# Contiguous first transfers, dt's one-source steps on ScalarE, and a two-phase transfer rate in the planner of a hybrid SSD and attention layer

## The chip, the cores and the metric

The kernel runs on one core of a Trainium2 chip. The metric is device time of one execution in microseconds (us); lower is better. The times are medians of several runs.

The engines are named as the profile names them: PE is TensorE (matmuls and transposes), DVE is VectorE, ACT is ScalarE, POOL is GpSimd, SP is SyncE, which here only issues transfers.

## The reference

One layer of a bidirectional encoder over 512 tokens of 1024 channels, float32. Cut to what matters:

```python
h = rmsnorm(x, pre_mix_norm)
z, xbc, dt_raw, q, k, v, gates = split_cols(h @ w_in, IN_SPLITS)   # 2048, 4096, 64, 1024, 256, 256, 2048
# SSD branch, chunks of 128 tokens, a scan forward and one backward, 32 heads each
xbc = silu(depthwise_conv(xbc) + conv_b)
dt  = softplus(dt_raw + dt_bias)             # 512 tokens x 64 (two directions)
cs  = cumsum(dt * -exp(a_log)) in each chunk # decay tables come from cs
y_ssd = gated_rmsnorm(y_fwd + y_bwd + xs * d_skip, z, ssd_norm) @ w_ssd_out
# attention, 16 query heads, 4 key heads, window +-128, relative bias, a sink logit for each head
y_attn = window_attention(q, k, v, sink, rel_bias_table) @ w_attn_out
mixed = (sigmoid(g_ssd) * y_ssd + sigmoid(g_attn) * y_attn) @ w_o
x = x + rmsnorm(mixed, post_mix_norm)
f = square(relu(rmsnorm(x, pre_mlp_norm) @ w_mlp_in)) @ w_mlp_out
out = x + rmsnorm(f, post_mlp_norm)
```

The part of the kernel that the change touches is the beginning: the norm's scale, the V and dt columns of the first projection, softplus and the sums over dt.

## The kernel before

**Products.** Every float32 operand of a large product is split into a high and a low part that PE can take at full rate. For a weight tile `wr` of 128x1024, ACT casts the high part `wh` (L496) and POOL subtracts to get the low part `wl` in four instructions of 128x256 (L500). A product is then three matmuls (`mm3`): high by high, low by high, high by low. All matmuls stand on line L421 and all transposes on L425, which are helpers.

**Stages at the start.** `start` (L637) loads the tokens in two forms. `xt` is a transposed copy of the first 256 tokens, in eight pieces k of 128 channels by 256 tokens; ACT and DVE multiply each by the norm's weight `gT` (L661, L663) to `xg`, and PE forms V and dt of the first two token tiles from it in plain float32, before the row scales exist. `x` is the tokens by row in eight transfers (L679); ACT (L687) and DVE (L688) form sums of squares, POOL the row scale (L690, L691), ACT and DVE the scaled tokens (L724, L725), and PE transposes those of the last two tiles. For the first two, PE spreads the row scales over the partitions by a product with a diagonal tile `dg`, and the split parts `h` follow on DVE (L707), ACT (L709) and POOL (L710). `v_quanta` loads the V and dt columns `wv` in three pieces of 2, 3 and 3 k (`V_CHUNKS`), the first on ACT's queue and the others on SP's (L584), and splits them (L588, L591).

**Softplus.** `dt_math` (L777) works on 128x256 tiles named `dtw`: max(v, 0) + log(1 + exp(-|v|)), the logarithm by a series in s = e / (e + 2). The steps are |v| and exp on ACT (L787, L788), e + 2 (L789), its reciprocal (L790), the product (L791), the square (L792), the first factor 1/17 (L793), seven Horner steps (L795), a last one (L796), max(v, 0) (L797), dt (L798) and dt by -exp(a_log) (L800), all on DVE. `sums` follows: cumulative sums by PE, a copy `cs` (L810), its negative `ncs` (L811), the decay tables (L813 to L816).

**After them.** `kv_quanta` projects K, of which ACT makes `KH` (L848, L850) and DVE `KL` (L849); `q_quantum` makes Q (L875 on ACT, L876 on DVE). Attention for each key head k is scores (L899 on DVE), maximum (L905), exp (L908), sums (L909 to L911), division (L914), transposes `pT` (L925). Each conv block of the SSD branch is four DVE steps (L976) and a silu (L982, L983). `L1147` multiplies the masks `m` of the scan, and the scan's outputs are products of `m` and `x`.

**Order.** The instructions are first written by quanta, then `Planner.plan` runs a model of the engines over all of them: durations by shape, a lock between DVE and POOL, and one queue of transfers with a rate. It takes for each engine the instruction that is ready and due first, and PE's order comes out of it too, within rules. `chain` then fixes the order so found on every engine. A tile's free buffer counts as well: three raw weight tiles, three split ones, three PE banks named `pp` and five named `ps`. The transfers in the model:

```python
                queue = max(queue, t + 900) + size / RATE
                free[e], end = end, queue + LAND
```

Here `t` is the time of issue in ns, `RATE` is 340 bytes for each ns, and `LAND` 2500 ns.

Of the kernel before, what the change touches and what calls it, by code (L numbers as in the profile page):

```python
# [12 lines left out]
AF = mybir.ActivationFunctionType  # L13
ALU = mybir.AluOpType
# [8 lines left out]
C_Z, C_X, C_B, C_C, C_DT = 0, 2048, 4096, 5120, 6144  # L23
C_Q, C_K, C_V, C_GS, C_GA = 6208, 7232, 7488, 7744, 8768
# [9 lines left out]
BACK = 3  # L34
WARM = 8
V_CHUNKS = ((0, 2), (2, 5), (5, 8))
COLD = 7000.0
RATE, LAND = 340, 2500

OUTPUT = 350  # L40

# [23 lines left out]
def packed(given):  # L65

    rows = lambda n: given[n].reshape(-1, 128)
    by_partition = lambda a: np.ascontiguousarray(a.reshape(8, 128, -1).transpose(1, 0, 2).reshape(128, -1))
    cv = np.concatenate([rows(n) for n in ("conv_w", "conv_b", "b_gate", "ssd_norm", "pre_mlp_norm")]).T
    row = np.concatenate([given[n].reshape(-1) for n in ("dt_bias", "a_log", "attn_sink", "d_skip")])  # L70
    bucket, far = buckets()
    bias = np.ascontiguousarray(given["rel_bias_table"][bucket].T)
    bias[:, far] = NEG
    w = given["w_in"][0]
    return {"cv": np.ascontiguousarray(cv), "row": row, "bias": bias,
            "gt": np.ascontiguousarray(rows("pre_mix_norm").T), "xt": by_partition(given["x"][0, :256].T),
            "wv": by_partition(np.concatenate([w[:, C_V:C_V + 256], w[:, C_DT:C_DT + 64]], axis=1))}


class Slots:  # L80
# [5 lines left out]
    def get(self, name, shape=(128, 512), dtype=F32):  # L86
        s = self.free.popleft()
        self.n += 1
        t = self.pool.tile(list(shape), dtype, tag=f"s{s}", name=f"{name}_{self.n}", bufs=1)
        self.tags[t.tensor.name] = f"s{s}", 1  # L90
        self.slot[id(t)] = (s, t)
        return t
# [6 lines left out]
class Planner:  # L99
# [184 lines left out]
    def plan(self, wait=0.3):  # L284
        late = self.deadlines()
        left = [len(p) + len(q) for p, q in zip(self.pre, self.turn)]
        ready = [0.0] * len(self.ins)
        done = [math.inf] * len(self.ins)
        avail = {e: [] for e in self.OVERLAP}
        key = [n if self.eng[n] == "PE" else late[n] for n in range(len(self.ins))]  # L290
        for n, k in enumerate(left):
            if not k:
                avail[self.eng[n]].append(n)
        free = dict.fromkeys(self.OVERLAP, 0.0)
        port = {"DVE": 0.0, "POOL": 0.0}
        queue, kind, landed = 0.0, None, deque([0.0] * 8)
        order = {e: [] for e in self.OVERLAP}
        for _ in self.ins:
            best = None
            for e, some in avail.items():  # L300
                if some:
                    t = max(free[e], min(ready[n] for n in some))
                    if best is None or t < best[0]:
                        best = t, e
            t, e = best
            some = avail[e]
            if e == "PE":
                n = self.next_matmul(some, ready, done, t, kind)
            else:
                n = min((n for n in some if ready[n] <= t), key=lambda n: (key[n], n))  # L310
                m = min(some, key=lambda n: (key[n], n))
                if ready[m] <= t + wait * self.cost[n][0]:
                    n = m
            some.remove(n)
            order[e].append(n)
            t = max(t, ready[n])
            c, locks = self.cost[n]
            if e == "PE" and t < COLD:
                c *= 2
            end = t + c  # L320
            if e == "SP" or "DMA" in type(self.ins[n]).__name__:
                aps = self.operands(self.ins[n].outs)
                size = 4 * math.prod(d[1] for d in aps[0].ap)
                queue = max(queue, t + 900) + size / RATE
                free[e], end = end, queue + LAND
                landed.append(end)
                landed.popleft()
                free["SP"] = max(free["SP"], min(landed) + 60)
            elif e == "PE":
                end += self.change(kind, self.kind[n])  # L330
                kind = self.kind[n]
                free[e], end = end, end + 160
            else:
                if locks:
                    other = "POOL" if e == "DVE" else "DVE"
                    end += max(0.0, port[other] - t - 145)
                    port[e] = end
                free[e] = end - self.OVERLAP[e]
            done[n] = end
            for s in self.post[n]:  # L340
                same = self.eng[s] == e == "PE"
                ready[s] = max(ready[s], free[e] if same else end + self.AFTER[self.eng[s]])
                left[s] -= 1
                if not left[s]:
                    avail[self.eng[s]].append(s)
            for s in self.next[n]:
                ready[s] = max(ready[s], t)
                left[s] -= 1
                if not left[s]:
                    avail[self.eng[s]].append(s)  # L350
        self.length = max(free.values())
        return order
# [10 lines left out]
class Trunk:  # L363
# [204 lines left out]
    def v_quanta(self):  # L568

        nc = self.nc  # L570
        get = self.slots.get
# [4 lines left out]
        def chunk(k0, k1):  # L576
            kk = k1 - k0
            raw = []

            def loads():  # L580
                r = self.wp.tile([128, 1024], F32, tag="wr", name=self.name("wr"), bufs=RAW)
                self.tags[r.tensor.name] = "wr", RAW
                raw.append(r[:, :kk * 320].rearrange("p (k n) -> p k n", k=kk))
                (nc.sync if k0 else nc.scalar).dma_start(r[:, :kk * 320], self.d_wv[:, k0 * 320:k1 * 320])  # L584

            def make():
                hi, lo = (t[:, :kk * 320].rearrange("p (k n) -> p k n", k=kk) for t in self.weight_parts())
                nc.scalar.copy(hi, raw[0])  # L588
                for k in range(kk):
                    e = nc.vector if k % 2 == 0 else nc.gpsimd  # L590
                    e.tensor_tensor(lo[:, k], raw[0][:, k], hi[:, k].bitcast(F32), op=ALU.subtract)  # L591
                return raw[0], hi, lo

            return loads, make, False
# [42 lines left out]
    def start(self):  # L637
        nc = self.nc
        get, put = self.slots.get, self.slots.put
        self.gT = self.const("gT", [128, 8])  # L640
        nc.scalar.dma_start(self.gT, self.d_gt)
        self.ident = self.const("ident", [128, 128])
        self.at(0, lambda: nc.scalar.dma_start(self.ident, self.d_cst[:, :128]))
        self.mhalf = self.const("mhalf", [128, 1])
        nc.vector.memset(self.mhalf, -0.5)
        self.ssq0 = self.const("ssq0", [128, 8])
        self.rst0 = self.const("rst0", [128, 4])
        ones = self.const("ones0", [128, 128])
# [2 lines left out]
        for _ in range(WARM):  # L651
            self.mm(pg[:, :128], ones, ones, True, True)
        self.h = [(get("h", dtype=F32R), get("h", dtype=F32R)) for _ in range(8)]
        xt, xg = ([get(n) for _ in range(4)] for n in ("xt", "xg"))
        cols = lambda a: [a[k // 2][:, k % 2 * 256:(k % 2 + 1) * 256] for k in range(8)]
        self.xg, xs = cols(xg), cols(xt)
        for k in range(8):
            if k % 2 == 0:
                nc.sync.dma_start(xt[k // 2], self.d_xt[:, k * 256:(k + 2) * 256])
            if k % 2:  # L660
                nc.scalar.activation(self.xg[k], xs[k], AF.Copy, scale=self.gT[:, k:k + 1])  # L661
            else:
                nc.vector.tensor_scalar(self.xg[k], xs[k], self.gT[:, k:k + 1], None, op0=ALU.mult)  # L663
        put(*xt)
        for t in range(2):
            xt = self.load_tokens(t)
# [110 lines left out]
    def dt_math(self):  # L777
# [8 lines left out]

        nc.scalar.activation(e, v, AF.Abs)  # L787
        nc.scalar.activation(e, e, AF.Exp, scale=-1.0)  # L788
        nc.vector.tensor_scalar(r, e, 2.0, None, op0=ALU.add)  # L789
        nc.vector.reciprocal(r, r)  # L790
        nc.vector.tensor_tensor(e, e, r, op=ALU.mult)  # L791
        nc.vector.tensor_tensor(s2, e, e, op=ALU.mult)  # L792
        nc.vector.tensor_scalar(p, s2, 1.0 / 17, None, op0=ALU.mult)  # L793
        for n in (15, 13, 11, 9, 7, 5, 3):
            nc.vector.scalar_tensor_tensor(p, p, 1.0 / n, s2, op0=ALU.add, op1=ALU.mult)  # L795
        nc.vector.scalar_tensor_tensor(p, p, 1.0, e, op0=ALU.add, op1=ALU.mult)  # L796
        nc.vector.tensor_scalar(v, v, 0.0, None, op0=ALU.max)  # L797
        nc.vector.scalar_tensor_tensor(self.dt, p, 2.0, v, op0=ALU.mult, op1=ALU.add)  # L798
        nc.scalar.activation(bias[:, 1], bias[:, 1], AF.Exp)
        nc.vector.scalar_tensor_tensor(al, self.dt, -1.0, bias[:, 1].unsqueeze(1).to_broadcast([128, 4, 64]),  # L800
# [2 lines left out]
        def sums():  # L803
# [4 lines left out]
            pt = self.bank("ps")  # L808
            self.mm(pt[:, :256], self.ones, al, True, True)
            nc.vector.tensor_copy(self.cs, pc3)  # L810
            nc.vector.tensor_scalar(self.ncs, self.cs, -1.0, None, op0=ALU.mult)  # L811
            pt3 = pt[:, :256].rearrange("p (c h) -> p c h", c=4)
            nc.scalar.activation(self.dec, pt3, AF.Exp)  # L813
            nc.vector.tensor_tensor(self.coef, pt3, self.cs, op=ALU.subtract)
# [885 lines left out]
```

## Time and profile before

| | us |
|---|---|
| median of 3 runs | 1090.57 |
| lowest, highest | 1088.97, 1091.22 |
| the profiled execution's own time | 1093.82 |
| its span in the trace | 1092.0 |

The granted PE clock of the profiled execution is 0.998 of full speed. Over the span PE is busy for 98%, POOL for 73%, DVE for 69%, ACT for 58%, and the core moves 122 GB/s on average, 267 GB/s in the first fortieth of the span.

A row of the timeline reads: start, duration, engine, line, operation, what it writes and reads with shapes, how many instructions were joined in the row, and in brackets how long the engine stood idle before it and who released it. A row of a line's summary gives the least, the median and the greatest duration in ns. A row of PE's waits gives who waited for whom: sum, times, longest. Several engines work at once, so an idle engine costs time only if PE, which is the fullest, has to wait in the end.

### The profile page before, as it was taken

The numbers are of one execution on the slowest core, as the hardware profiler recorded it, in microseconds if no ns is written. First come the engines' busy times: TensorE is split into PE (matmuls) and PEld (weight loads), VectorE is DVE, ScalarE is ACT, GpSimd is POOL, SyncE is SP. The second block draws the span as 40 slices with busy tenths as digits, with TensorE's granted clock in tenths as the row PEclk, the third lists the DMA queues.
The fourth block names the chain that finished last, engine by engine and source line by source line (L and its number), as shares of the span: only waits on it lengthen the run. The fifth ranks groups of instructions, "written<-read, shape, count | busy, mean of one in ns | idle before, by whom it ended". The sixth has DMA issues, their size and how long they took to land.

```text
span 1092.0 us, 16583 instructions
## 1 busy us (share of the span) xinstructions
PE 1072.8 (98%) x5542; PEld 896.6 (82%) x5542; DVE 755.2 (69%) x1284; ACT 637.7 (58%) x1372; POOL 799.0 (73%) x986
## 2 busy tenths in 40 slices
PE   8998999999999999999999999999999999999997
PEld 7787888888888888787888888888888888888885
DVE  5877788787687687888787753334572583583698
ACT  6556777686676777676678533323654544444552
POOL 4736566567658798988989976521588898898994
PEclk9999999999999999999999999999999999999999
DMA  8334433534445536354645563534222422424232
GB/s 267 99 94 128 126 88 103 147 91 121 114 105 135 138 101 165 99 148 122 170 127 142 148 187 108 162 102 161 83 75 69 149 83 82 149 81 139 98 97 77
DMA packets 208181, 133.20 MB, mean 122 GB/s; under 512 B 9688, under 2 KB 190168, under 8 KB 208096
## 3 DMA queue, kind: packets, MB, share of 16 engines
q1 hardware_dynamic: 207664, 131.75, 43.0%
q8 instruction: 43, 0.70, 0.3%
q10 hardware_dynamic: 432, 0.40, 0.1%
q14 instruction: 42, 0.34, 0.1%
HBM read 127.63 MB, written 4.49 MB: 121 GB/s over the span
## 4 chain that ended last, share of the span: by engine, by line
PE 85%; DVE 6%; DMA 5%; ACT 2%; issue 1%; POOL 1%; SPq 0%; DVEq 0%; POOLq 0%; ACTq 0%
PE pp L421 59%; PE ps L421 23%; PE ps L425 3%; DMA rstd<-rrow 2%; DMA rf<-csT 1%; DVE yT L1219 1%; DVE dtw L797 1%; DVE u L976 1%; DMA wr<-in_wv 1%; DMA rrow<-rcol 1%; DMA rcol<-rrow 1%; ACT wh L496 0%; DVE m L1146 0%; DVE dtw L795 0%; SPq L1119 0%
## 5 line engine op out<-in xcount | busy, mean ns | idle before, releaser
L500 POOL TENSOR_TENSOR wl<-wr,wh 128x256 fp32r<-128x256 f32 (+1 forms) x500 | 421.4, 871 | 154.8 <-ACT wh L496 141.4
L421 PE MATMUL pp<-h,wh 128*128 128x512 f32 (+1 forms) x1712 | 524.9, 388 | 1.4 <-ACT KH L850 1.4
L421 PEld LDWEIGHTS pp<-h,wh 128*128 128x128 f32 x1712 | 316.2, 188 | 65.7 <-ACT KH L850 1.9
L421 PE MATMUL pp<-h,wl 128*128 128x512 f32 (+1 forms) x856 | 331.9, 388 | 0.0
L496 ACT CAST wh<-wr 128x1024 fp32r<-128x1024 f32 x131 | 136.4, 1041 | 141.7 <-PE pp L421 119.8
L421 PEld LDWEIGHTS pp<-h,wl 128*128 128x128 f32 x856 | 160.8, 188 | 32.0 <-issue 0.2
L1536 POOL TENSOR_TENSOR wl<-wd,wh 128x256 fp32r<-128x256 f32 x158 | 129.8, 859 | 12.1 <-ACT wh L1533 12.0
L1533 ACT CAST wh<-wd 128x512 fp32r<-128x512 f32 x82 | 47.3, 618 | 30.1 <-PE ps L421 15.8
L421 PE MATMUL ps<-wh,fl 128*128 128x512 f32 x164 | 63.8, 389 | 0.0
L421 PE MATMUL ps<-wl,fh 128*128 128x512 f32 x164 | 63.8, 389 | 0.0
L421 PE MATMUL ps<-wh,fh 128*128 128x512 f32 x164 | 63.8, 389 | 0.0
L1144 ACT ACTIVATE n<-cb,tables 128x128 f32<-128x128 f32 x128 | 49.4, 390 | 19.0 <-DVE cb L1135 16.8
L1403 DVE SCALAR_TENSOR_TENSOR pp<-pp,r 128x512 f32<-128x512 f32 (+1 forms) x31 | 17.6, 567 | 57.0 <-ACT r L1400 56.8
L976 DVE SCALAR_TENSOR_TENSOR u<-pp,cv,u 128x510 f32<-128x510 f32 (+1 forms) x64 | 47.7, 745 | 6.7 <-ACT u L972 5.4
L1145 ACT ACTIVATE m<-cb,tables 128x128 f32<-128x128 f32 x128 | 49.0, 388 | 3.9 <-DVE cb L1135 3.9
L421 PE MATMUL pp<-yh,wl 128*128 128x512 f32 x128 | 49.9, 390 | 0.0
L421 PE MATMUL pp<-yl,wh 128*128 128x512 f32 x128 | 49.8, 389 | 0.0
L421 PE MATMUL pp<-yh,wh 128*128 128x512 f32 x128 | 49.7, 389 | 0.0
L1140 ACT ACTIVATE rf<-rf,tables 128x128 f32<-128x128 f32 x128 | 42.3, 391 | 12.6 <-DMA rf<-csT 12.6
L908 ACT ACTIVATE P<-P,mx 128x384 f32<-128x384 f32 (+1 forms) x64 | 35.2, 552 | 18.4 <-DVE mx L905 18.4
L1138 POOL TENSOR_TENSOR rb<-rb,tables 128x512 f32<-128x512 f32 x32 | 33.6, 1054 | 14.7 <-DMA rb<-csT 10.9
L1074 POOL TENSOR_TENSOR xd<-x,tables 128x256 f32<-128x256 f32 x48 | 33.5, 719 | 12.0 <-ACT x L999 10.1
(269 smaller groups left out, 2170.9 us busy)
## 6 DMA issues: line engine op xcount, KB each, us to landing
wr<-in_w_in SPq DMA_DIRECT2D x74, 512.0 KB, 4.1
wr<-in_w_mlp_in SPq DMA_DIRECT2D x32, 512.0 KB, 4.1
wd<-in_w_mlp_out SPq DMA_DIRECT2D x64, 256.0 KB, 4.9
rf<-csT SPq DMA_DIRECT2D x32, 256.0 KB, 4.8
rb<-csT SPq DMA_DIRECT2D x32, 256.0 KB, 3.9
wr<-in_w_ssd_out SPq DMA_DIRECT2D x14, 512.0 KB, 4.2
E<-csE SPq DMA_DIRECT2D x96, 64.0 KB, 3.5
x<-in_x SPq DMA_DIRECT2D x16, 256.0 KB, 5.3
```

The costliest lines, as they stand in the source:

```text
L421: self.nc.tensor.matmul(out, lhsT, rhs, start=start, stop=stop, skip_group_check=more)
L496: self.nc.scalar.copy(hi[:, :m], raw)
L500: engines[e].tensor_tensor(lo[:, c], raw[:, c], hi[:, c].bitcast(F32), op=ALU.subtract)
L908: nc.scalar.activation(p[:, :w], p[:, :w], AF.Exp, bias=mx[:, n:n + 1], accum_out=sm[:, n:n + 1])
L976: nc.vector.scalar_tensor_tensor(u[:, a:e], ps[:, a + d:e + d], self.wtap(t, b), u[:, a:e], op0=ALU.mult, op1=ALU.add)
L1074: nc.gpsimd.tensor_tensor(v4(xd[:, d * 256:(d + 1) * 256]), v4(xs(c)), by_dir(self.coef, c)[:, d].unsqueeze(2).to_broadcast([128, 4, 64]), ...
L1138: nc.gpsimd.tensor_tensor(v4(rb), v4(rb), cs[:, 1].unsqueeze(2).to_broadcast([128, 4, 128]), op=ALU.subtract)
L1140: nc.scalar.activation(v4(rf)[:, h], v4(rf)[:, h], AF.Identity, bias=ncs[:, 0, h:h + 1])
L1144: nc.scalar.activation(v4(n)[:, h], cb[:, 0], AF.Copy, scale=dt[:, 0, h:h + 1])
L1145: nc.scalar.activation(v4(m)[:, h], cb[:, 1], AF.Copy, scale=dt[:, 1, h:h + 1])
L1533: nc.scalar.copy(hi, src)
L1536: (nc.vector if q == 512 else nc.gpsimd).tensor_tensor(lo[:, c], src[:, c], hi[:, c].bitcast(F32), op=ALU.subtract)
```

## The change

Three things are changed together.

1. `xt` and `wv` are laid out so that each transfer reads one stretch of memory. `gT`'s eight columns ride at the head of the first piece of `xt`, and `xt` comes in five pieces (1, 2, 2, 2 and 1 k) in place of four of 2. The separate transfer of `gT` on ACT's queue is gone. A small copy into `rst0` on ACT stands at the front of its row.
2. In `dt_math`, five steps with one source go from DVE to ACT: e + 2, the square, the factor 1/17, max(v, 0) and `ncs`. The constant 2.0 for the bias is a new tile `two`.
3. In `plan`, the rate is 350 for transfers issued in the first 12000 ns of the model, and 260 afterwards, in place of 340.

```diff
+X_CHUNKS = ((0, 1), (1, 3), (3, 5), (5, 7), (7, 8))
-RATE, LAND = 340, 2500
+RATE, EARLY, LAND = 260, 350, 2500
...
-                queue = max(queue, t + 900) + size / RATE
+                queue = max(queue, t + 900) + size / (EARLY if t < 12000 else RATE)
...
-                (nc.sync if k0 else nc.scalar).dma_start(r[:, :kk * 320], self.d_wv[:, k0 * 320:k1 * 320])
+                (nc.sync if k0 else nc.scalar).dma_start(
+                    r[:, :kk * 320], self.d_wv[k0 * 320 * 128:k1 * 320 * 128].rearrange("(p n) -> p n", p=128))
...
-        nc.scalar.dma_start(self.gT, self.d_gt)
+        self.two = self.const("two", [128, 1])
+        nc.vector.memset(self.two, 2.0)
...
-        xt, xg = ([get(n) for _ in range(4)] for n in ("xt", "xg"))
-        cols = lambda a: [a[k // 2][:, k % 2 * 256:(k % 2 + 1) * 256] for k in range(8)]
-        self.xg, xs = cols(xg), cols(xt)
-        for k in range(8):
-            if k % 2 == 0:
-                nc.sync.dma_start(xt[k // 2], self.d_xt[:, k * 256:(k + 2) * 256])
-            if k % 2:
-                nc.scalar.activation(self.xg[k], xs[k], AF.Copy, scale=self.gT[:, k:k + 1])
-            else:
-                nc.vector.tensor_scalar(self.xg[k], xs[k], self.gT[:, k:k + 1], None, op0=ALU.mult)
+        nc.scalar.copy(self.rst0, self.mhalf.to_broadcast([128, 4]))
+        xt, xg = ([get(n) for _ in range(m)] for n, m in (("xt", 5), ("xg", 4)))
+        self.xg = [xg[k // 2][:, k % 2 * 256:(k % 2 + 1) * 256] for k in range(8)]
+        at = 0
+        for x, (k0, k1) in zip(xt, X_CHUNKS):
+            n = (k1 - k0) * 256 + (8 if k0 == 0 else 0)
+            nc.sync.dma_start(x[:, :n], self.d_xt[at:at + 128 * n].rearrange("(p n) -> p n", p=128))
+            at += 128 * n
+            if k0 == 0:
+                nc.vector.tensor_copy(self.gT, x[:, :8])
+            for k in range(k0, k1):
+                c, g = n - (k1 - k) * 256, (self.gT[:, k:k + 1] if k else x[:, :1])
+                if k % 2:
+                    nc.scalar.activation(self.xg[k], x[:, c:c + 256], AF.Copy, scale=g)
+                else:
+                    nc.vector.tensor_scalar(self.xg[k], x[:, c:c + 256], g, None, op0=ALU.mult)
...
-        nc.vector.tensor_scalar(r, e, 2.0, None, op0=ALU.add)
+        nc.scalar.activation(r, e, AF.Identity, bias=self.two)
...
-        nc.vector.tensor_tensor(s2, e, e, op=ALU.mult)
-        nc.vector.tensor_scalar(p, s2, 1.0 / 17, None, op0=ALU.mult)
+        nc.scalar.activation(s2, e, AF.Square)
+        nc.scalar.activation(p, s2, AF.Copy, scale=1.0 / 17)
...
-        nc.vector.tensor_scalar(v, v, 0.0, None, op0=ALU.max)
+        nc.scalar.activation(v, v, AF.Relu)
...
-            nc.vector.tensor_scalar(self.ncs, self.cs, -1.0, None, op0=ALU.mult)
+            nc.scalar.activation(self.ncs, self.cs, AF.Copy, scale=-1.0)
```

The changed kernel's lines have other numbers: L797 to L816 of the kernel before are L807 to L826, and helper lines shift by two.

The order changes with it. On DVE in the softplus stage, the row before the change (`dtw` are its tiles, `KL` is the low part of K, `pp` a PE bank):

```order
L604 TENSOR_TENSOR dtw_71<-ps_294,row 128x64
L797 TENSOR_SCALAR dtw_71<-dtw_71 128x256
L789 TENSOR_SCALAR dtw_372<-dtw_371 128x256
L790 RECIPROCAL dtw_372<-dtw_372 128x256
L849 TENSOR_TENSOR KL_430<-pp_404,KH_429 64x512
L791 TENSOR_TENSOR dtw_371<-dtw_371,dtw_372 128x256
L792 TENSOR_TENSOR dtw_373<-dtw_371 128x256
L849 TENSOR_TENSOR KL_436<-pp_404,KH_435 64x512
L793 TENSOR_SCALAR dtw_374<-dtw_373 128x256
L795 SCALAR_TENSOR_TENSOR dtw_374<-dtw_374,dtw_373 128x256 x5
```

and the same place after it (L607 is L604, L859 is L849, L805 is L795):

```order
L607 TENSOR_TENSOR dtw_71<-ps_299,row 128x64
L800 RECIPROCAL dtw_377<-dtw_377 128x256
L801 TENSOR_TENSOR dtw_376<-dtw_376,dtw_377 128x256
L859 TENSOR_TENSOR KL_435<-pp_409,KH_434 64x512
L859 TENSOR_TENSOR KL_441<-pp_409,KH_440 64x512
L805 SCALAR_TENSOR_TENSOR dtw_379<-dtw_379,dtw_378 128x256 x5
```

Four DVE instructions are gone between the dt sum and the Horner steps, and both KL stand ahead of the Horner steps.

On SP at the start, the transfers before the change (`xt` transposed tokens, `wr` pieces of V's weights, `x` tokens by row):

```order
L659 DMA xt_106<-in_xt 128x512
L659 DMA xt_107<-in_xt 128x512
L584 DMA wr_150<-in_wv 128x960
L659 DMA xt_108<-in_xt 128x512
L584 DMA wr_152<-in_wv 128x960
L659 DMA xt_109<-in_xt 128x512
L679 DMA x_200<-in_x 128x512
```

and after it:

```order
L664 DMA xt_108<-in_xt 128x264
L664 DMA xt_109<-in_xt 128x512
L586 DMA wr_155<-in_wv 128x960
L664 DMA xt_110<-in_xt 128x512
L664 DMA xt_111<-in_xt 128x512
L586 DMA wr_157<-in_wv 128x960
L664 DMA xt_112<-in_xt 128x256
L689 DMA x_205<-in_x 128x512
```

The third piece of V's weights now has 264 + 3 x 512 columns of `xt` ahead of it on SP, in place of 3 x 512.

On PE at about 450 us, the row before the change (`pp` projections of `h`, `ps` with `m` and `x` outputs of the scan, `ps_5332` the transposes of the conv block B):

```order
L421 MATMUL pp_5292<-h_102,wh_5112 128x512
L421 MATMUL pp_5292<-h_103,wh_5112 128x512
L421 MATMUL pp_5292<-h_102,wl_5113 128x512
L421 MATMUL pp_5292<-h_104,wh_5112 128x512
L421 MATMUL pp_5292<-h_105,wh_5112 128x512
L421 MATMUL pp_5292<-h_104,wl_5113 128x512
L425 MATMUL ps_5332<-ident,B_5167 128x128 x4
L421 MATMUL pp_5350<-h_90,wh_5178 128x512
```

and after it (names are five higher, so `pp_5297` is `pp_5292`, and `ps_5337` is `ps_5332`):

```order
L423 MATMUL pp_5297<-h_94,wh_5117 128x512
L423 MATMUL pp_5297<-h_93,wl_5118 128x512
L423 MATMUL ps_5231<-m_5063,x_4597 64x128 x4
L423 MATMUL ps_5231<-m_5141,x_4597 64x128 x4
L427 MATMUL ps_5337<-ident,B_5172 128x128 x4
L423 MATMUL pp_5297<-h_95,wh_5117 128x512
L423 MATMUL pp_5297<-h_96,wh_5117 128x512
```

B's transposes stood behind the whole projection; now they stand behind its first six matmuls, 18 matmuls earlier, and a piece of the scan's outputs has moved next to them from 12 matmuls ahead.

More of the change, by code (lines that the diff above doesn't have):

```diff
@@ L67, in packed @@
     rows = lambda n: given[n].reshape(-1, 128)
-    by_partition = lambda a: np.ascontiguousarray(a.reshape(8, 128, -1).transpose(1, 0, 2).reshape(128, -1))
+    xt, wv = given["x"][0, :256].T.reshape(8, 128, 256), np.concatenate(
+        [given["w_in"][0][:, c:c + n].reshape(8, 128, n) for c, n in ((C_V, 256), (C_DT, 64))], axis=2)
+    pieces = lambda a, cuts: np.concatenate([a[k0:k1].transpose(1, 0, 2).reshape(-1) for k0, k1 in cuts])
     cv = np.concatenate([rows(n) for n in ("conv_w", "conv_b", "b_gate", "ssd_norm", "pre_mlp_norm")]).T
@@ L73, in packed @@
     bias[:, far] = NEG
-    w = given["w_in"][0]
+    first = np.concatenate([rows("pre_mix_norm").T, xt[0]], axis=1)
     return {"cv": np.ascontiguousarray(cv), "row": row, "bias": bias,
-            "gt": np.ascontiguousarray(rows("pre_mix_norm").T), "xt": by_partition(given["x"][0, :256].T),
-            "wv": by_partition(np.concatenate([w[:, C_V:C_V + 256], w[:, C_DT:C_DT + 64]], axis=1))}
+            "xt": np.concatenate([first.reshape(-1), pieces(xt, X_CHUNKS[1:])]), "wv": pieces(wv, V_CHUNKS)}
 class Slots:
```

## The prediction

> **What bounds the kernel now.** I read the page's shares first, then TensorE's own waits, then the timelines of the other engines around each of them.
>
> ```profile
> PE 1072.8 (98%) x5542; PEld 896.6 (82%) x5542; DVE 755.2 (69%) x1284; ACT 637.7 (58%) x1372; POOL 799.0 (73%) x986
> 6.59 9.02 PE L421 MATMUL ps<-wr,xg 128*128 128x320 f32 x32 [1.77 <-DMA wr<-in_wv]
> 15.98 0.44 PE L425 MATMUL pp<-ident,x 128*128 128x128 f32 x2 [0.37 <-ACT x L724]
> 44.49 0.72 PE L421 MATMUL pp<-h,wh 128*128 128x512 f32 x2 [1.45 <-ACT KH L850]
> 51.12 0.39 PE L421 MATMUL ps<-KH,Q 128*128 128x256 f32 x1 [0.89 <-DVE Q L876]
> 84.99 0.45 PE L421 MATMUL ps<-KH,Q 128*128 128x384 f32 x1 [2.86 <-ACT pT L925]
> ```
>
> TensorE (PE) is busy for 98% of the span, and the change leaves its matmuls as they are. So only a hole in its row can be gained, and a new hole is what can be lost. The three holes at 44, 51 and 85 us are 1.45 + 0.89 + 2.86 = 5.20. They look unrelated: one waits for K, one for Q, one for a transposed P. VectorE's (DVE's) timeline, with ScalarE (ACT) and GpSimd (POOL) beside it, shows one source for the first two:
>
> ```profile
> 25.93 5.63 POOL L710 TENSOR_TENSOR h<-hf,h 128x256 fp32r<-128x256 f32 x8
> 31.52 7.70 POOL L500 TENSOR_TENSOR wl<-wr,wh 128x256 fp32r<-128x256 f32 x11
> 30.23 0.42 ACT L788 ACTIVATE dtw<-dtw 128x256 f32<-128x256 f32 x1
> 30.23 9.13 DVE L797 TENSOR_SCALAR dtw<-dtw 128x256 f32<-128x256 f32 x1 [0.48 <-ACT dtw L787]
> 39.28 0.28 DVE L789 TENSOR_SCALAR dtw<-dtw 128x256 f32<-128x256 f32 x1
> 39.60 1.75 DVE L790 RECIPROCAL dtw<-dtw 128x256 f32<-128x256 f32 x1
> 41.27 0.62 DVE L849 TENSOR_TENSOR KL<-pp,KH 64x512 fp32r<-64x512 f32 x1
> 41.92 0.58 ACT L850 CAST KH<-pp 64x512 fp32r<-64x512 f32 x1 [7.98 <-DVE KL L849]
> ```
>
> L797 is v = max(v, 0), one source, 128x256. It lasts 9.13 us; L789, of the same operation and shape, takes 0.28. POOL runs without a gap from 25.93 until its eleven L500 splits end at 39.22, and L797 ends at 39.36. So L797 stood until POOL's queue ran dry, and 9.13 - 0.28 = 8.85 us of DVE were lost. Everything behind it is late: the reciprocal, KL at 41.27, ACT's KH (which stood for 7.98), then PE at 44.49.
>
> **dt's steps on ScalarE.** The new rows on ACT are 128x256 activations, 0.42 each by L788. DVE's L789, L792, L793, L797 and the later L811 go. Walking the stage by these durations: Exp (L788) still ends at 30.65, the relu and "+2" take ACT 2 x 0.42 to 31.5, the reciprocal takes 1.75 to 33.25, and L791, with two sources, 0.85 to 34.1. KL then follows at 34.1 in place of 41.27, and the second KL by 37.1 once ACT and PE have fed it. For the Horner steps and the rest:
>
> ```profile
> L795 DVE SCALAR_TENSOR_TENSOR dtw<-dtw,dtw x7: 424/426/852, 44.2 to 47.9; 128x256 f32<-128x256 f32 x7
> L811 DVE TENSOR_SCALAR tables<-tables x1: 816/816/816, 62.4 to 62.4; 128x256 f32<-128x256 f32 x1
> L905 DVE TENSOR_SCALAR mx<-mx x16: 154/307/686, 55.6 to 327.5; 128x4 f32<-128x4 f32 x16
> L911 DVE RECIPROCAL sm<-sm x16: 167/178/180, 59.2 to 331.2; 128x4 f32<-128x4 f32 x16
> 47.08 1.66 DVE L795 SCALAR_TENSOR_TENSOR dtw<-dtw,dtw 128x256 f32<-128x256 f32 x2
> ```
>
> A two-source step takes 0.43 alone and 0.85 with POOL at work. I take 0.85 for the five that now start at 37.1: to 41.4. Two more, L796, L798, KL and the two Q at the shown 0.7 to 0.85 put both Q at about 47.5, while PE without these holes, and with 0.3 from the start (below), reaches the scores at 51.12 - 0.89 - 1.45 - 0.3 = 48.5. So the holes of 1.45 and 0.89 both go: **2.34**. ACT's five extra rows, 2.1 us, lie where ACT stood for 7.98 and cost nothing; without that cover (the chain still late) each would delay KH by 0.42.
>
> This price rests on the stall not finding another victim. The other one-source rows beside POOL, L905 and L811, waited at most 0.53 and about 0.54 over their short time. [...]
>
> **The third hole** hangs on a chain in which DVE and ACT hand work to each other without rest:
>
> ```profile
> 53.58 0.48 DVE L899 CUSTOM_DVE_ANT_0 P<-ps,bt,row 128x256 f32<-128x256 f32 x1
> 56.30 1.04 PE L421 MATMUL ps<-dtw,cst 128*128 128x128 f32 x6
> 58.90 0.42 DVE L810 COPY tables<-ps 128x256 f32<-128x256 f32 x1
> 72.30 0.48 DVE L899 CUSTOM_DVE_ANT_0 P<-ps,bt,row 128x256 f32<-128x256 f32 x1
> 84.56 0.37 ACT L925 COPY pT<-ps 128x256 f32<-128x256 f32 x1
> ```
>
> The first score row of DVE (53.58) starts 2.46 after PE's first score matmul (51.12). With DVE free in time it would start about 0.45 behind it, one score matmul and its handover, so against PE's row the chain moves 2.0 ahead. It can't move more: L810 copies what PE wrote from 56.30 to 57.34, and stands 1.6 to 1.9 behind that now. I take **2.0** of the 2.86, leaving a hole of 0.9. The bounds are 1.7 and the whole 2.86 (L811 off DVE adds 0.82, which could fetch the rest).
>
> **The start.** The transfers' bytes ahead of the token tiles are the same within 3 KB; what changes is their cut. PE starts plain V when wv's first piece lands (6.59), which now leaves ACT's queue first.
>
> ```profile
> 5.12 1.28 ACT L661 ACT_TABLE_LOAD   x1 [5.12 <-DMA xt<-in_xt]
> 11.72 1.56 DVE L591 TENSOR_TENSOR wl<-wr,wh 128x320 fp32r<-128x320 f32 x2
> 13.21 0.68 DVE L688 CUSTOM_DVE_ANT_0 junk<-x 128x512 f32<-128x512 f32 x1
> 13.38 0.63 ACT L687 ACTIVATE junk<-x 128x512 f32<-128x512 f32 x1 [0.63 <-DMA x<-in_x]
> 0.00:20.00 20.00, 16.45 (x74) 12.52 (x75) 10.18 (x25) 11.54 (x24) 8.62 (x17) 1.00 0.91 298
> ```
>
> An earlier first matmul and the 1.28 table load taken off the way do not reach the end: at 15.98 PE waits again, for the normalised tokens, and these wait for landed x (13.38) with the transfer engines 91% busy. wv's third piece has 134 KB more of xt ahead of it than before, at 298 GB/s 0.45 us later; its DVE split (11.72) would then push L688 (13.21). Against that stands the loss of 128 small rows of gT at the head. I take 0, between 0.5 better and 0.6 worse.
>
> **The planner's rate.** With another transfer rate the planner writes 47 pieces of PE's order elsewhere, all between about 138 and 643 us apart from a few near the start. Near the start both row-scale broadcasts now stand side by side and POOL writes the eight h one split, 0.70, earlier. Eight POOL rows of 5.63 / 8 = 0.704 pace a projection:
>
> ```profile
> 26.19 1.03 PE L421 MATMUL pp<-h,wh 128*128 128x512 f32 x3
> 28.68 0.63 PE L421 MATMUL pp<-h,wh 128*128 128x512 f32 x2
> 29.39 0.63 PE L421 MATMUL pp<-h,wh 128*128 128x512 f32 x2
> 72.47 0.62 PE L421 MATMUL pp<-h,wh 128*128 128x512 f32 x2
> 73.15 0.62 PE L421 MATMUL pp<-h,wh 128*128 128x512 f32 x2
> ```
>
> A step takes 0.71 there and 0.68 elsewhere: 8 x 0.03 = 0.24, with a little at 26.19; I take **0.3**, from 0 to 0.6. The rest of the new order I cost at nothing, from 1 better to 1 worse, by these rows:
>
> ```profile
> PE ps L421 <- DVE m L1147: 1.6, 2, 1.0
> PE ps L425 <- DVE u L983: 0.9, 1, 0.9
> PE ps L425 <- DVE P L914: 0.3, 1, 0.3
> 449.20 1.14 DVE L983 SCALAR_TENSOR_TENSOR B<-th,B 128x512 f32<-128x512 f32 x1
> 454.93 0.60 PE L425 MATMUL ps<-ident,B 128*128 128x128 f32 x4
> ```
>
> All of today's waits behind 85 us are 1.6 + 0.9 + 0.3 = 2.8 in four places, 0.7 each. B's transposes, shown in the order above, move 18 rows (18 x 0.227 = 4.1 us) ahead, to about 450.8; B is ready at 450.34. That still fits, with 0.5 to spare.
>
> **Sum.** 2.34 + 2.0 + 0 + 0.3 = 4.64. The profiled execution (1093.82, of which the span is 1092.0) becomes 1089.2. It lies 3.25 above the median of 1090.57, and the same gain makes 1085.9 of the median. About 0.2%, 2.2 us, is what a measurement of this kernel can tell from no change.
>
> **Forecast, 0.64:** 1085.9. Its own range, all bad bounds (2.34 + 1.7 + 0 - 0.6 - 1 = 2.4) to all good (2.34 + 2.86 + 0.6 + 0.5 + 1 = 7.3): 1083.3 to 1088.1.
>
> **Rival, the stall takes the reciprocal, 0.09.** DVE's first instruction under POOL's unbroken row is now the one-source reciprocal at 31.5. If it waits as L797 did, it ends at 39.4 to 41.0 in place of 41.35; with two DVE steps fewer behind it (0.42 + 0.29) the chain gains 1.0 to 2.7, the first hole shrinks and the third stays: some 1.0 in all, 1089.6. Against it, L911 keeps to 167 to 180 ns everywhere, and 1753 ns for 256 elements is slow, ordinary work. [...]
>
> **Rival, the third hole is bound elsewhere, 0.11.** If ACT's casts between 60 and 84 and not DVE's lateness set 84.56, the 2.86 stays, and with 0.5 lost in the start the gain is 2.34 + 0.3 - 0.5 = 2.1: 1088.4. The continuous handover up to 84.56 speaks against it.
>
> **Rival, slower: the new order, 0.16.** PE takes its rows in order, so a piece set ahead of its producer stops everything. The planner sets margins like the 0.5 above by modelled durations; where DVE or POOL run late by a doubled step (0.43 to 0.85), such a margin is gone. If 14 of the 47 pieces wait for today's mean of 0.7, that is 9.8 in place of 2.8, 7.0 more: 7.0 - 4.64 = 2.4 slower, 1092.9. It turns from a gain at 4.64 more of waits, nine to ten places. For it: four such places exist today. Against: they came from an order drawn in the same way, and cost 2.8 in 535 us.
>
> That the change doesn't remove the stall at all is in the first rival.
>
> **Numbers.** Faster by over 0.2% (below 1088.4): the forecast and half of the third-hole case, 0.70. Within: the reciprocal case and the other half, 0.14. Slower: 0.16. The range of 1082.5 to 1090.5 holds the first three cases with their bounds and leaves out the slower one.
>
> **What would show it.** No one-source DVE row over 1 us between 30 and 40; the reciprocal near 31.5 with 1.75; KH no longer waiting for 8 us; no PE wait near 44 and 51, and about 0.9 near 80; PE's first real wait still for L724's tokens near 16. It is wrong if a DVE row lasts until POOL's chain ends, if the wait before the transposes grows past 1, or if the sum of PE's waits between 138 and 643 us exceeds 5.

## The result, and the profile after

The changed kernel's median is 1085.55 us (1084.45 to 1090.15, 20 runs) against 1089.73 of the kernel before on the same chip (20 runs): a ratio of 0.9963, 95% interval 0.9949 to 0.9976, that is 4.0 us faster (2.6 to 5.6). The forecast was 1085.9. The two profiled executions lie further apart, 1093.82 and 1087.15, since the one of before lies 4.1 us above its kernel's median.

The page's shares of the changed kernel, and PE's longest waits behind its first matmul:

```profile
PE 1072.1 (99%) x5542; PEld 897.3 (83%) x5542; DVE 742.0 (68%) x1281; ACT 641.8 (59%) x1378; POOL 801.2 (74%) x986
PE ps L423 <- DVE m L1157: 1.0, 1, 1.0
PE ps L423 <- ACT pT L935: 0.9, 1, 0.9
PE ps L423 <- ACT sh L440: 0.9, 1, 0.9
PE ps L423 <- ACT xg L671: 0.6, 1, 0.6
PE ps L427 <- DVE P L924: 0.5, 1, 0.5
```

PE has the same matmuls and is busy for the same time; only waits went. The three holes of 5.20 at 44, 51 and 85 us have no successor. Behind 100 us the waits are 3.57 against 2.77. The timeline of the start and of the softplus stage (POOL, DVE, then PE):

```profile
30.34 9.32 POOL L502 TENSOR_TENSOR wl<-wr,wh 128x256 fp32r<-128x256 f32 x12
30.41 1.75 DVE L800 RECIPROCAL dtw<-dtw 128x256 f32<-128x256 f32 x1 [1.64 <-ACT dtw L799]
32.20 0.56 DVE L801 TENSOR_TENSOR dtw<-dtw,dtw 128x256 f32<-128x256 f32 x1
32.68 0.67 DVE L859 TENSOR_TENSOR KL<-pp,KH 64x512 fp32r<-64x512 f32 x1
35.76 4.19 DVE L805 SCALAR_TENSOR_TENSOR dtw<-dtw,dtw 128x256 f32<-128x256 f32 x5
4.61 3.97 PE L423 MATMUL ps<-wr,xg 128*128 128x320 f32 x10
9.14 6.19 PE L423 MATMUL ps<-wr,xg 128*128 128x320 f32 x22 [0.56 <-ACT xg L671]
15.53 0.44 PE L427 MATMUL pp<-ident,x 128*128 128x128 f32 x2 [0.20 <-ACT x L734]
```

The walk of the prediction is there nearly row for row: the reciprocal keeps its 1.75 beside an unbroken POOL row, KL comes at 32.7 in place of 41.27, the five Horner steps take 4.19 (4.25 was counted). On the face of it the reasons held. The experiments show that most of them did not.

### The profile page after: what moved, and what is told of

It is laid out like the page before. It is cut to its first block, busy times and chain, and to the rows that moved or that the text cites. A ratio compares the mean times of both kernels' runs of the same rounds, so it can differ in the third digit from the quotient of the medians.

```text
span 1085.4 us, 16598 instructions
## 1 busy us (share of the span) xinstructions
PE 1072.1 (99%) x5542; PEld 897.3 (83%) x5542; DVE 742.0 (68%) x1281; ACT 641.8 (59%) x1378; POOL 801.2 (74%) x986
## 5 line engine op out<-in xcount | busy, mean ns | idle before, releaser
L1543 ACT CAST wh<-wd 128x512 fp32r<-128x512 f32 x82 | 47.3, 618 | 32.4 <-PE ps L423 16.2
L1190 POOL TENSOR_TENSOR w<-w,E 128x256 f32<-128x256 f32 x48 | 37.9, 802 | 14.3 <-DVE w L1186 13.0
```

The lines of the kernel that those rows point to most:

```text
L1190: nc.gpsimd.tensor_tensor(wc, wc, E[:, d], op=ALU.add)
L1543: nc.scalar.copy(hi, src)
```

## The experiments

One table carries them. "Transposes" is the start of PE's first token transposes, which closes the start; "DVE row" the longest DVE instruction begun between 27 and 42 us; "holes" PE's waits from 25 to 100 us and "late" those behind 100 us, each of 0.13 us or more. Times in us; each row is one profile, and the ratio that of the timed runs to the kernel before in the same session (its median was 1089.7 to 1094.0 by session).

| layout | rate | dt steps | transposes | DVE row | holes | late | ratio (95%) |
|---|---|---|---|---|---|---|---|
| old | old | DVE (before) | 15.98 | 9.13 | 5.20 | 2.77 | 1 |
| old | old | relu with two sources | 18.18 | 9.26 | 5.30 | 4.83 | 0.9992 (0.9963 to 1.002) |
| old | old | three steps with two sources | 17.24 | 1.75 | 0 | 4.43 | 0.9996 (0.9973 to 1.0018) |
| old | old | DVE, one POOL instruction later | 18.20 | 1.75 | 0 | 2.95 | 0.9983 (0.9953 to 1.0013) |
| old | old | ACT | 15.76 | 6.30 | 1.95 | 4.86 | 1.0002 (0.9978 to 1.0026) |
| old | new | DVE | 16.89 | 9.06 | 2.50 | 2.15 | 0.9966 (0.9938 to 0.9993) |
| new | old | DVE | 15.34 | 1.75 | 0 | 4.57 | 0.9966 (0.9939 to 0.9994) |
| new | old | ACT | 15.18 | 6.46 | 2.11 | 4.36 | 0.9978 (0.9952 to 1.0004) |
| new | new | ACT (the change) | 15.53 | 1.75 | 0 | 3.57 | 0.9963 (0.9949 to 0.9976) |
| new | new | ACT, again | 15.33 | 1.75 | 0 | 0.91 | 0.993 (0.9902 to 0.9958) |
| new | new | relu on DVE | 15.29 | 1.75 | 0 | 2.96 | 0.9939 (0.9917 to 0.9961) |
| new | new | DVE | 15.34 | 1.75 | 0 | 1.64 | 0.9925 (0.9901 to 0.9949) |
| new | new | DVE, again | 14.93 | 1.75 | 0 | 1.90 | 0.9913 (0.9882 to 0.9945) |

**Is it the one-source form?** The relu alone, in place, written with two sources:

```diff
-        nc.vector.tensor_scalar(v, v, 0.0, None, op0=ALU.max)
+        nc.vector.scalar_tensor_tensor(v, v, 0.0, v, op0=ALU.max, op1=ALU.max)
```

> The kernel before, with L797 alone written with two sources on VectorE, max(max(v, 0), v); TensorE's, GpSimd's and the transfers' orders are those of before. Theory A (a one-source VectorE instruction starves while GpSimd's row has no gap): L797 takes about 0.85 us, and the next one-source row, e + 2 at L789, which starts at about 31.1 under the same GpSimd row, takes its place and stands for some 8 us until that row ends near 39.2; the three TensorE holes (1.45, 0.89, 2.86) stay and the time is within 0.5 us of before. Rival B (something of L797 itself, such as its reading and writing one tile): L789 keeps to 0.28 us, the holes at 44 and 51 us go, and the time falls by 2.3 to 5.2 us.

DVE's timeline of that kernel:

```profile
32.02 9.26 DVE L797 SCALAR_TENSOR_TENSOR dtw<-dtw 128x256 f32<-128x256 f32 x1 [0.48 <-ACT dtw L787]
41.21 0.28 DVE L789 TENSOR_SCALAR dtw<-dtw 128x256 f32<-128x256 f32 x1
```

Neither theory: the two-source row stands for 9.26 us, and the one-source row behind it runs in 0.28, by which time POOL's row is over. Then three steps with two sources (e + 2 as max(e + 2, e), the factor as min(s / 17, s)):

```diff
+        nc.vector.scalar_tensor_tensor(r, e, 2.0, e, op0=ALU.add, op1=ALU.max)
+        nc.vector.scalar_tensor_tensor(p, s2, 1.0 / 17, s2, op0=ALU.mult, op1=ALU.min)
```

> The kernel before, with L797, L789 and L793 written with two sources, all still on VectorE and at the same places; TensorE's, GpSimd's and the transfers' orders are those of before. Theory A: no VectorE row between 30 and 40 us lasts over 1.8 us, the reciprocal starts near 32 and takes 1.75, KL comes near 34.6 in place of 41.27, the holes at 44 and 51 us go and that at 85 shrinks to at most 0.9: 4.3 us faster (from 2.3 to 5.2), ratio about 0.996. Rival B (VectorE as a whole is held while GpSimd runs without a gap, whatever its instruction): some row, the reciprocal or another, lasts until GpSimd's row ends near 39, and the gain is under 1.5 us. Rival C (the work had to leave VectorE): the holes stay by half, gain about 2.

```profile
31.07 0.91 DVE L797 SCALAR_TENSOR_TENSOR dtw<-dtw 128x256 f32<-128x256 f32 x1 [0.48 <-ACT dtw L787]
31.91 0.96 DVE L789 SCALAR_TENSOR_TENSOR dtw<-dtw 128x256 f32<-128x256 f32 x1
```

The same L797 that stood for 9.26 takes 0.91 here, and the holes are gone from this profile; yet the timed runs gain nothing (0.9996). Last, one source put back into the changed kernel:

```diff
-        nc.scalar.activation(v, v, AF.Relu)
+        nc.vector.tensor_scalar(v, v, 0.0, None, op0=ALU.max)
```

> The changed kernel with one of the five moved steps, max(v, 0), put back on VectorE with one source; TensorE's, GpSimd's and the transfers' orders are those of the changed kernel. Theory A: that row starts near 30 us and stands until GpSimd's row ends near 39.6; the three holes come back with 1.5, 0.9 and 2.9 and the time is 4 to 5.5 us longer than the changed kernel's, ratio 0.999 to 1.001 against before. Rival D (the layout or the planner's rate brought the gain): it stays within 1 us of the changed kernel, ratio about 0.997.

```profile
29.02 0.56 DVE L807 TENSOR_SCALAR dtw<-dtw 128x256 f32<-128x256 f32 x1 [0.49 <-ACT dtw L797]
30.13 9.34 POOL L502 TENSOR_TENSOR wl<-wr,wh 128x256 fp32r<-128x256 f32 x12
```

It runs in 0.56 beside POOL, and the time stays that of the changed kernel. The form does not decide.

**Is it the move to ScalarE?** The five steps alone moved, all else as before:

> The kernel before with only the five dt steps moved to ScalarE (the planner then draws its order with the old rate). Theory A: the three holes go or shrink as in the changed kernel, 4.3 to 5.2 us faster, ratio 0.995 to 0.996; the start stays as before, with plain V at 6.59 and transposes at 15.98. Rival D: a gain of at most 1 us, ratio over 0.999.

```profile
31.16 1.75 DVE L792 RECIPROCAL dtw<-dtw 128x256 f32<-128x256 f32 x1 [1.64 <-ACT dtw L791]
32.95 6.30 DVE L793 TENSOR_TENSOR dtw<-dtw,dtw 128x256 f32<-128x256 f32 x1
39.17 0.67 DVE L851 TENSOR_TENSOR KL<-pp,KH 64x512 fp32r<-64x512 f32 x1
31.27 7.69 POOL L500 TENSOR_TENSOR wl<-wr,wh 128x256 fp32r<-128x256 f32 x11
```

The stall took the product e times r (L793 here) and ended 0.29 behind POOL's row, at 39.25. It is later and shorter than before, and its holes are 1.95 in place of 5.20; but the time is that of before, as rival D had it.

**The parts apart.** The layout alone, the rate alone, both without dt, and the change with the old rate. The edit of the last, cut to what matters:

```diff
-RATE, EARLY, LAND = 260, 350, 2500
+RATE, LAND = 340, 2500
```

> The kernel before with only the new layout of tokens and V weights (first piece small, no transfer of gT, table load in front); old rate, dt on VectorE. Theory L (the start gains): the first transposes come 0.5 to 0.8 us earlier than before's 15.98 in the mean and with less spread, ratio about 0.999. Theory S (a lottery at the GpSimd row decides a stall of one VectorE row, one source or two): a stall may stand here or not; if not, the holes at 44, 51 and 85 us are missing from the profile, whatever the form. Theory R (the planner's new rate brings most of the gain in the waits between 380 and 650 us): those waits stay at 2.5 to 5 us.

> The kernel before with only the planner's rate in two phases. Theory R: the waits between 380 and 650 us fall to about 2 us, 2 to 3 us faster, ratio 0.997 to 0.998, also where the stall at 30 us stands. Theory D (the dt steps alone gain): within 0.5 us of before, ratio 0.9995 to 1.0005.

> The changed kernel with the planner's old rate of 340 throughout. Theory R: the waits between 380 and 650 us are back at 2.5 to 5 us and the time is 2 to 3 us longer than the changed kernel's, ratio about 0.999 against before. Theory D: as fast as the changed kernel, ratio 0.996.

> The changed kernel with all five dt steps back on VectorE. Theory R with L: nearly the whole gain stays, ratio 0.996 to 0.9975; if the profile shows a stalled VectorE row near 30 us its holes of 3 to 5 us stand in it, and if not they don't. Theory D: the gain is gone, ratio 0.999 to 1.000.

Layout and rate gain 0.34% each, with wide intervals, and together without any dt step on ACT they give 1085.93 (0.9925). The change with the old rate has the stall again, in L801 of its profile:

```profile
31.93 6.46 DVE L801 TENSOR_TENSOR dtw<-dtw,dtw 128x256 f32<-128x256 f32 x1
```

The layout alone, with the one-source relu on DVE, has none (0.92 us). The transposes come 0.64 earlier with it, as theory L said. PE's waits between 380 and 650 us are 1.25 with the rate alone, 4.3 with the layout alone and 4.0 in the change with the old rate, against 2.5 before, as theory R said; the time of the last run can't tell R from D.

The rate alone shows what may be a further cost of the stall, which the column of holes leaves out. PE waits 2.50 for KH, and from 47.3 to 50.7 its matmuls of 128x512 start 0.43 apart, before and behind that 0.23. The last line below is the stretch from 46 to 52 us: busy time and instructions of PE, PEld (weight loads), DVE, ACT and POOL, then granted clock, DMA share and GB/s.

```profile
45.96 0.73 PE L421 MATMUL pp<-h,wh 128*128 128x512 f32 x2 [2.50 <-ACT KH L850]
47.68 1.05 PE L421 MATMUL pp<-h,wh 128*128 128x512 f32 x2
51.80 0.62 PE L421 MATMUL pp<-h,wh 128*128 128x512 f32 x2
46.00:52.00 6.00, 6.00 (x19) 4.78 (x20) 5.68 (x11) 5.87 (x9) 3.70 (x5) 0.72 0.00 1
```

That is some 1.5 us more. That the hole brings it is argued from its place only: the profile with the two-source relu has such a spell behind its hole of 2.84; that of before, with 2.86, has none.

**The dt steps, side by side.** The changed kernel and its version with dt on DVE, on one chip:

> The changed kernel once more, for a comparison on one chip with the version that has its dt steps on VectorE. Theory P (layout and rate bring the gain, the dt steps nothing in the mean): 1085.5 to 1087, equal to the other within 1 us. Theory D (the dt steps are worth their 2 to 5 us): it is faster than the other by 2 us or more.

> The changed kernel with all five dt steps back on VectorE, once more, beside the changed kernel. Theory P: equal to it within 1 us, and no VectorE row over 2 us between 28 and 40 us. Theory D: 2 us or more slower.

1085.04 and 1084.85 us: equal. With the new layout and rate, moving dt's steps brings nothing that can be measured.

**The pair by itself.** VectorE beside GpSimd, in a kernel that computes nothing of the layer:

```python
for form in (one_source, two_sources, product, reciprocal):
    for i in range(40):
        nc.scalar.copy(wh, wr)                   # releases GpSimd's row of eight
        for j in range(8): nc.gpsimd.tensor_tensor(wl[j % 4], wr[j % 4], wh[j % 4], op=ALU.subtract)
        nc.scalar.activation(v[:, :240 + 20 * i], src[:, :240 + 20 * i], AF.Copy, scale=1.0)
        form()                                   # VectorE on v[:, :256]
```

> A measurement by itself; it computes nothing of the layer. 160 times GpSimd runs eight 128x256 subtractions without a gap (some 5.6 us) and VectorE starts one 128x256 instruction into that row, in 40 steps of about 0.016 us; four forms: one source, two sources, a product of two tiles, a reciprocal. Theory S1 (which start meets the stall depends on the moment within a GpSimd instruction): in a part of the 40 starts, next to one another, the first three forms last until GpSimd's row ends (2 to 5 us), and elsewhere under 1 us; the reciprocal stays at 1.75. Theory S2 (the form decides): all 40 of the one-source form last long and the others never. Theory S3 (an outside cause, such as transfers under way): no row lasts over 1.2 us, the reciprocal's 1.75 aside.

The summaries of its four DVE lines (least, median, greatest ns) and three of its turns:

```profile
L29 DVE TENSOR_SCALAR v<-v x40: 293/505/860, 6.4 to 267.9; 128x256 f32<-128x256 f32 x40
L32 DVE SCALAR_TENSOR_TENSOR v<-v x40: 424/652/993, 273.9 to 541.0; 128x256 f32<-128x256 f32 x40
L35 DVE TENSOR_TENSOR v<-v,u x40: 424/652/993, 547.1 to 814.2; 128x256 f32<-128x256 f32 x40
L38 DVE RECIPROCAL v<-v x40: 1752/1753/1754, 820.3 to 1080.1; 128x256 f32<-128x256 f32 x40
12.78 0.60 DVE L29 TENSOR_SCALAR v<-v 128x256 f32<-128x256 f32 x1 [6.09 <-ACT v L46]
273.68 5.66 POOL L45 TENSOR_TENSOR wl<-wr,wh 128x256 fp32r<-128x256 f32 x8 [1.15 <-ACT wh L42]
273.94 0.74 DVE L32 SCALAR_TENSOR_TENSOR v<-v 128x256 f32<-128x256 f32 x1 [5.39 <-ACT v L46]
280.50 5.67 POOL L45 TENSOR_TENSOR wl<-wr,wh 128x256 fp32r<-128x256 f32 x8 [1.15 <-ACT wh L42]
280.78 0.73 DVE L32 SCALAR_TENSOR_TENSOR v<-v 128x256 f32<-128x256 f32 x1 [6.09 <-ACT v L46]
```

Each of the first three forms takes at most 0.57 us over its own 0.29 or 0.42, less than one POOL instruction (5.66 / 8 = 0.71); the reciprocal never waits (1752 to 1754 ns). The two-source rows shown begin 0.26 and 0.28 us behind the start of POOL's row and end 1.00 and 1.01 behind it: less their own 0.42, both wait until about 0.58, near the end of POOL's first instruction, and run while POOL goes on to 5.66. That is not what the layer's rows of 6.3 to 9.3 us did. S1 and S2 fail here: none of the 40 starts and no form brings the stall about in these 120 rows. S3 forecast no row over 1.2 us, and the longest is 0.99, so something that this kernel leaves out must be there. Transfers, S3's example, are not needed: in the profile of before the transfer engines were 0.00 busy from 30 to 32 us, when L797 had begun to stand (the last three numbers are the granted clock, the DMA share and the GB/s):

```profile
30.00:32.00 2.00, 2.00 (x11) 1.37 (x10) 1.77 (x1) 0.62 (x2) 2.00 (x4) 1.00 0.00 0
```

**POOL's row.** In the seven profiles in which POOL writes five splits ahead of the eight h, a DVE row stands in five; in the five with four splits ahead, which only layout and rate together give, in none. With five, POOL's row runs into the eight h without a pause; with four it pauses some 0.24 us ahead of them. In the profile of before the five are:

```profile
22.42 3.55 POOL L500 TENSOR_TENSOR wl<-wr,wh 128x256 fp32r<-128x256 f32 x5 [2.31 <-ACT wh L496]
```

So the fifth split was moved by hand in the kernel before:

```diff
+        i = next(i for i, n in enumerate(pool) if any(r.startswith("hf") for r in reads(n)))
+        pool.insert(i + 7, pool.pop(i - 1))
```

> The kernel before (old layout, old rate, dt on VectorE) with one GpSimd instruction moved: the first split of the second weight tile goes from ahead of the eight h to behind them, as the changed kernel has it; the other engines' orders are those of before. Theory G (the moment at which VectorE's first dt row meets GpSimd's row decides, and this shift moves it): no VectorE row over 2 us between 28 and 40 us, the holes at 44, 51 and 85 us gone, 3 to 5 us faster than before, ratio 0.9955 to 0.9975. Rival H (the old layout or the old order of the other engines holds the stall): a row of some 9 us stands as in before, gain under 0.7 us, ratio about 0.9995.

```profile
27.53 5.70 POOL L715 TENSOR_TENSOR h<-hf,h 128x256 fp32r<-128x256 f32 x8 [0.45 <-ACT h L714]
32.03 0.59 DVE L802 TENSOR_SCALAR dtw<-dtw 128x256 f32<-128x256 f32 x1 [0.48 <-ACT dtw L792]
```

No stall and no hole, as theory G said: five of seven against none of six. In timed runs the gain is 1.9 us, from 5.1 to a loss of 1.4, and the medians are equal (1090.59 and 1090.32), so how often the stall strikes outside a profile is not settled. One rival was not tested, the length of POOL's unbroken row. The five rows that stalled met its 12th or 16th instruction. In the other eight profiles DVE's first dt row of 128x256, the reciprocal aside, met the 7th or the 11th, and once the 12th (three steps with two sources). In the kernel without the layer POOL's row is eight long and DVE meets the first or the second.

## Why the prediction was right, and where its steps were not

**Holes only.** Right for the pair: PE's busy time is 1072.1 after 1072.8. Not for every kernel here: with the two-source relu it is 1077.7, where eleven matmuls of the start took 0.53 us in place of 0.27 and others were slow behind a hole, which the prediction does not count.

**"dt's steps on ScalarE", 2.34.** The step that failed. In the pair of profiles both holes went, and the walk to KL was good to 1.5 us. But the stall does not hang on these steps: moved to ACT under the old rate they leave it to the product (6.30, 6.46), left on DVE under the new layout and rate the relu and e + 2 run in 0.56 to 0.83. That is the first rival with another victim than the reciprocal. What the steps do where the stall strikes is to make it cheaper, 2.0 us of holes instead of 5.2. The prediction took one profile of before as the kernel's habit.

**The third hole, 2.0 of 2.86.** Undersized: it went wholly in the pair and in all eight profiles without a stall. With a stall of 6.3 or 6.5 it is half there, as in the kernel with only dt moved:

```profile
81.46 0.44 PE L421 MATMUL ps<-KH,Q 128*128 128x384 f32 x1 [1.48 <-ACT pT L927]
```

It is missing beside the rate alone's stall of 9.06 too: there PE, late by its hole of 2.50 and the matmuls 0.43 apart, reaches these scores at 83.59 and not at 81.64, and DVE's second score row comes 1.07 earlier. So the hole is the chain's lateness against PE, as the prediction reckoned it, and it goes as well when PE is late.

**The start, 0 (from 0.6 worse to 0.5 better).** Mis-sized, and outside its bounds. In the pair the transposes come 0.45 earlier and the V stage behind them 0.75, of which 0.53 is left at the first projection (26.19, then 25.66). Over the profiles they start at 17.04 in the mean of the six with the old layout (15.76 to 18.20), at 15.28 in the seven with the new (14.93 to 15.53): 1.8 us, and little spread. The profile of before was one of the two good ones of six. V's 32 plain matmuls, and two stretches of 6 us around them, in the kernel with a two-source relu:

```profile
6.48 11.87 PE L421 MATMUL ps<-wr,xg 128*128 128x320 f32 x32 [1.66 <-DMA wr<-in_wv]
6.00:12.00 6.00, 5.52 (x11) 3.59 (x12) 3.99 (x8) 5.17 (x10) 3.22 (x3) 1.00 1.03 398
12.00:18.00 6.00, 6.00 (x23) 4.22 (x22) 4.14 (x11) 3.41 (x10) 4.04 (x9) 1.00 1.10 346
```

The same 32 took 9.02 in the profile of before. Eleven matmuls fill the first window and 23 the second: the early ones take 0.53 us each, the others 0.27 (those of the split parts, of the same shape, 0.15 from start to start in the profile of before), while the granted clock reads 1.00 in both. In the six old-layout profiles 0, 0, 5, 5, 11 and 11 of them are slow; in the new layout at most three. There PE goes on within 0.51 us of its first products (of a constant tile `ones`) instead of waiting for 1.7 to 2.2. That this is the reason is argued and not shown: among the six the wait of 2.19 left no slow matmul and that of 1.66 left eleven. What slows them was not found; they cost 11 x 0.26 = 2.9 us at most. In the mean 4.6 fewer are slow in the new layout, 1.2 of the 1.8 us; the prediction counted the earlier first matmul at nothing.

**The pacing, 0.3.** 0.12 in the pair.

**The planner's order, 0 (1 better to 1 worse).** In the pair 0.8 worse, inside. Over all profiles the waits behind 100 us are 4.1 in the mean of seven with the old rate (2.77 to 4.86), 2.2 in six with the new (0.91 to 3.57): 1.9 better. Two profiles of one kernel differ by more than the pair does (the changed kernel's 3.57 and 0.91). By the means the term was mis-sized, and on the good side: the slower rival, 0.16, has nothing for it. PE's waits with only dt moved, old rate:

```profile
PE ps L421 <- DVE m L1149: 2.3, 3, 1.5
PE ps L425 <- DVE u L985: 1.6, 1, 1.6
```

and in the changed kernel, run again, the largest one behind 100 us:

```profile
PE ps L423 <- ACT sh L440: 0.4, 1, 0.4
```

**The sum.** 4.64 was forecast and 4.0 came (2.6 to 5.6), but from other terms: layout and rate, about 1.8 and 1.9 in the profiles, make 3.7 without the dt steps. The number was right by compensation; the stall's 4.3 was the largest term, and dt's part in the timed gain is nothing. It was right by luck of the session too. Measured again on another chip, the same pair gave 0.993, 7.6 us faster (4.6 to 10.7): the changed kernel repeated (1085.04) and the kernel before did not (1092.16). Of its runs 2 of 20 lie above 1095 us in the first session and 9 of 19 in that one; of the 60 runs of all kernels with the new layout and the new rate, none lies above 1090.2. The 3.7 of the profiles does not account for that.

**Open.** What starts the stall: not the form, not the pair of engines alone; POOL's order goes with it in 13 profiles, and the trigger was not found. How often it strikes in unprofiled runs. What lifts so many runs of the kernel before above 1095 us: the rate alone has none of 12 there although the stall stands in its profile, and neither has the kernel with one POOL instruction moved.

## What to carry to other kernels

A long row in one profile is one execution: profile a kernel several times before pricing its removal, and undo each part of a change before crediting it. The changed kernel with its dt steps left on VectorE is as fast and simpler. At the start, feed TensorE soon after its products of constants, even with a small first piece: all seven profiles that do so begin the transposes by 15.53 us.

## What the hardware showed beyond expectation

A VectorE instruction stood for 6.30 to 9.26 us in five of the 13 profiles, with one source or with two, while GpSimd ran 9 to 13 instructions past it, each at its usual 0.70, although the same pair, measured alone, shows no wait over 0.57 us in 120 rows. And PE took 0.53 us in place of 0.27 for up to 11 matmuls of the start with a granted clock of 1.00 in the rows; behind the rate alone's hole of 2.50 us its matmuls of 128x512 started 0.43 apart in place of 0.23, where the row read 0.72, and the two-source relu's profile has such a spell behind its hole of 2.84.
